# First pair of merge gates interleaved with the sums of blocks, and its block sums moved to GpSimd, in a bidirectional encoder layer on one core

## The chip, the cores and the metric

The kernel runs on one core of a Trainium2 chip. The core has a matrix engine (TensorE: PE, with its weight loads shown apart as PEld), a vector engine (VectorE: DVE), a scalar engine (ScalarE: ACT), a general engine (GpSimd: POOL) and an engine that here issues the DMAs (SyncE: SP). Each of them works through its own list of instructions in order; semaphores hold an instruction back until what it reads is there. SBUF is the on-chip memory that all engines use, PSUM the banks into which the matmuls accumulate. The metric is the device time of one execution in microseconds; the time of a kernel is the median of its runs. The profile is of one execution that the hardware profiler took.

## What is computed

One layer of an encoder with two parallel token mixers, a merge by gates and a SwiGLU block, 1024 tokens (and 16 learned ones in front) of 1024 values, all in float32:

```
h = rmsnorm(h_res, norm1_w[l])
proj = h @ w_in[l]
(q, k, v, z, b_raw, a_raw, sc_b, sc_c, sc_x, gate_a, gate_b) = jnp.split(proj, SPLIT_POINTS, axis=-1)
o_dn = gated_deltanet_bidir(q, k, v, z, b_raw, a_raw, dn_conv_w[l], A_log[l], dt_bias[l], dn_norm_w[l])
y_a = o_dn @ w_branch_dn[l]
y_b = (sc_b * depthwise_conv_centred(sc_c * sc_x, sc_conv_w[l])) @ w_branch_sc[l]
merged = jax.nn.sigmoid(gate_a) * y_a + jax.nn.sigmoid(gate_b) * y_b
h_res = h_res + merged @ w_out[l]
```

The change lies where the columns `z` (the last three of its eight units of 128 columns) and `gate_a`, `gate_b` (the last five of eight units) of `h @ w_in` are computed.

## The kernel before

**Arithmetic.** Every float32 matrix is held as two parts, `hi` and `lo`, and a product takes three matmuls: hi·hi, hi·lo, lo·hi. `split` (L100) makes the parts of a weight: ACT casts the raw tile to `hi` (L101), DVE subtracts to get `lo` (L102). `dense` (L129 to L136) is the plain product of one unit of weights with 512 tokens: 8 blocks of 128 rows, three matmuls each, 24 in all, into one PSUM bank.

**Stages.** The heads of the DeltaNet run first, then the part of the change, then the merge, the output projection and the SwiGLU block. The part of the change starts with three `z` units: `z_rows(h)` (L1496) makes a left and a right half of 512 tokens; for each, 24 matmuls, a tanh on ACT (L1502) and a `scalar_tensor_tensor` on DVE (L1504) that reads the bank and leaves the result in the tile `s`. They are called z0, z1 and z2 here.

Then come the gates, in pairs: pair n takes unit j = 3 + n of `gate_a` and of `gate_b`, for n = 0 to 4. A pair is done as a 2×2 block product with seven block products in place of eight (the scheme of Strassen in Winograd's form). Each block product (`product`, L1434) is 12 matmuls of 128×512. The stationary side is made from weights: the blocks A11, A12 (from the first unit) and A22 (from the second) as they are, and the block sums S1 to S4. The moving side is made from the tokens: B11, B21, B22 as they are, and the sums T1 to T4. Products that are added go into the same bank one after another (`add_to`), and between them ACT copies the bank (L1543 is the copy behind A12·B21 and S2·T2 of a pair, into a tile of four, `s4`).

- `moving_sums` (L1442) makes T1 to T4 from the token tiles `hTh` and `al`. T1 and T2 are formed in the two halves of the tile `mA`, T3 and a helper `d_` in the tile `b3`. DVE does the additions (L1409) and subtractions (L179), ACT the casts to `hi` (L1457), DVE the subtractions to `lo` (L179 too). T4 is formed over T1 once T2 and T3 are done, and its parts are put into `b3`.
- `sums` (L1414) makes S1 to S4 of a pair in place, in the raw weight tiles `rg` and `ru`: one addition (L1416) and three subtractions (L179) of 128×512 on DVE. `stationary2` (L1421) splits them into `mB` (even pairs) or `mA` (odd pairs). A11, A12 are split into `wh`, `wl`, A22 into `w2` (even) or `u_hl` (odd).
- `pair` (L1534) runs the seven products of a pair. For all but the last pair the order is A11·B11, A12·B21, S2·T2, S1·T1, S3·T3, S4·B22, A22·T4.

**Banks.** PSUM has three groups: two banks `pm` (`psm`), three `pe` (`psd`), three `pd` (`pss`). `psany` goes round all of them, `psz` round `pm` and `pe` only. A pair takes one `pd` bank, and two banks of `psz`.

**Order.** From the first `z` unit to the end of pair 0 the program is under a manual schedule for DVE, PE and ACT (`border0`, L1493 to L1617): these three do their work in the order in which it is written, whatever waits. That order is the run of `next(...)` calls at the end of the listing. After it, and for SP and POOL throughout, a scheduler sets the order.

Of the kernel before, what the change touches and what calls it, by code (L numbers as in the profile page):

```python
# [11 lines left out]
AF = mybir.ActivationFunctionType  # L12
# [6 lines left out]
KT = 8  # L19
# [29 lines left out]
def encoder_layer(ctx: ExitStack, tc: tile.TileContext, x, meta, norm1_w, w_in, w_ba,  # L49
# [128 lines left out]
    def sub(out, a, b):  # L178
        nc.vector.tensor_tensor(out=out, in0=a, in1=b, op=ALU.subtract)  # L179
# [856 lines left out]
    with tc.tile_pool(name="st", bufs=1) as st:  # L1036
# [374 lines left out]
    s_hl, u_hl = [None, None], [None, None]  # L1411
    mov = {}

    def sums(rg, ru, s2, s4_, s3, s1):  # L1414
        g0, g1, u0, u1 = rg[:, 0:4], rg[:, 4:8], ru[:, 0:4], ru[:, 4:8]
        nc.vector.tensor_tensor(out=s1, in0=u0, in1=u1, op=ALU.add)  # L1416
        sub(s3, g0, u0)
        sub(s2, s1, g0)
        sub(s4_, g1, s2)

    def stationary2(j, ru, sa, sb, A_):  # L1421

# [19 lines left out]
    def moving_sums():  # L1442

        c = [slice(C0 + META + 512 * i, C0 + META + 512 * i + 512) for i in range(2)]
        f = lambda m: m.bitcast(F32)
        h0, h1 = ([f(hx[0][:, 4 * i:4 * i + 4, cc]) for cc in c] for i in range(2))
        l0, l1, l2 = ([f(t[:, :, cc]) for cc in c] for t in low_tiles)
        for i in range(2):
            for j in range(2):
                mov[f"B{i + 1}{j + 1}"] = hx[0][:, 4 * i:4 * i + 4, c[j]], [hx[1][4 * i + k][:, c[j]] for k in range(4)]  # L1450
        for i, n in enumerate(("T1", "T2", "T3")):
            t = big(f"b{i}", [P, 2, 4, 512])
            mov[n] = t[:, 0], t[:, 1]
# [3 lines left out]
        high = lambda n, t: nc.scalar.copy(mov[n][0], t)  # L1457
# [12 lines left out]
        low_part("T2", t2)  # L1470
        yield
        sub(t3, h1[1], h0[1])
        sub(d_[:, a], l1[1], l0[1][:, a])
        sub(d_[:, b], l2[1], l0[1][:, b])
        add(t3, t3, d_)
        high("T3", t3)
        yield
        sub(t1, h1[0], t2)
        low_part("T3", t3)
        yield  # L1480
        t = big("b3", [P, 2, 4, 512])
# [14 lines left out]
    def z_rows(h):  # L1496

        sz = s4(SEQ)
        for sl in (left, right):
            po = psany()  # L1500
            dense(po, z_units[h - ZH], hx, C0 + META + sl.start, 512)
            nc.scalar.activation(sz[:, sl], po, AF.Tanh, scale=0.5)  # L1502
            yield
            nc.vector.scalar_tensor_tensor(out=sz[:, sl], in0=sz[:, sl], scalar=1.0, in1=po, op0=ALU.add, op1=ALU.mult)  # L1504
        nc.sync.dma_start(z_d[h], sz)
        yield
# [3 lines left out]
    def pair_weights(n, j):  # L1510

        s_hl[n % 2] = big(("mB", "mA")[n % 2], [P, 2, 2, KT, P])
        if n == 0:
            u = big("w2", [P, 2, 4, P])
            u_hl[0] = u[:, 0], u[:, 1]
        elif n == 1:
            u_hl[1] = [tp.tile([P, 4, P], F32R, tag="t2", name=uid("u_hl"), bufs=2) for _ in range(2)]
        gh, gl = wtiles([P, KT, P])
        rg, ru = (rawtile([P, KT, P]) for _ in range(2))
        nc.sync.dma_start(rg, w_in[unit(OGA + j * P)])  # L1520
        nc.sync.dma_start(ru, w_in[unit(OGB + j * P)])
# [5 lines left out]
        def second():  # L1527
            split(*u_hl[n % 2], ru[:, 4:8])
# [3 lines left out]
        return A_, first, second  # L1532

    def pair(n, j, A_, first, second):  # L1534

        last = j == KT - 1
        o1, o2 = s4(), s4()
        bank = pss()
        if not last:
            if n:  # L1540
                first()
            product(bank, A_["A11"], "B11")
            nc.scalar.copy(o1[:, left], bank)  # L1543
            po = psz()
            product(po, A_["A12"], "B21")
            add(o1[:, left], po, o1[:, left])
            half_turn(o1[:, left])
# [4 lines left out]
        bank2 = psz()
        if not last:
            product(bank, A_["S2"], "T2", True)
            nc.scalar.copy(o1[:, right], bank)
            product(bank2, A_["S1"], "T1")
            nc.scalar.copy(o2[:, right], bank2)
            product(bank, A_["S3"], "T3", True)
            add(o2[:, right], bank, o2[:, right])
            half_turn(o2[:, right])  # L1560
            product(bank2, A_["S4"], "B22", True)
            add(o1[:, right], bank2, o1[:, right])
            half_turn(o1[:, right])
            product(bank, A_["A22"], "T4", True)
            nc.scalar.activation(o2[:, left], bank, AF.Tanh, scale=0.5)
        else:
# [421 lines left out]
```

## Time and profile before

| | us |
|---|---|
| median of three runs | 2007.1 |
| the three runs | 2004.61, 2007.71, 2007.1 |
| the profiled execution, its own time | 2003.46 |
| its span (first to last instruction) | 2001.7 |
| PE busy in the span | 1974.2 |
| DVE busy | 1398.8 |
| ACT busy | 837.2 |
| POOL busy | 108.0 |

The span is what the profile covers; the time of an execution has 1.76 us more, which lie outside it. "Busy" is the time in which an engine had at least one instruction running. A timeline row has the start, the duration, the engine, the line, the operation with the tiles it writes and reads, and in brackets the idle time ahead of it with the instruction that ended it. A row of windows has the length of the window, then busy time and instruction count of PE, PEld, DVE, ACT and POOL, the granted clock of TensorE (1.00 is full), the share of the DMA engines and GB/s.

### The profile page before, as it was taken

How to read it: one execution, taken by the hardware profiler on the slowest of the kernel's cores; microseconds unless marked ns; L12 is line 12 of the kernel's file. 1: busy time of each engine (PE TensorE's matmuls, PEld its weight loads, DVE VectorE, ACT ScalarE, POOL GpSimd, SP SyncE). 2: the span in 40 equal slices, each digit the busy share in tenths (PEclk: the TensorE clock that was granted, in tenths of full speed). 3: DMA queues.
4: the chain of work that ended last, by engine and by line, in shares of the span. 5: the costliest groups of instructions: out<-in, count | busy, mean ns of one | idle time of the engine just before them, and what ended most of it. 6: DMA issues, size and time to landing. Idle time of an engine off the chain costs nothing.

```text
span 2001.7 us, 31862 instructions
## 1 busy us (share of the span) xinstructions
PE 1974.2 (99%) x11999; PEld 1720.7 (86%) x11999; DVE 1398.8 (70%) x3020; ACT 837.2 (42%) x1964; POOL 108.0 (5%) x407
## 2 busy tenths in 40 slices
PE   9999999999999999999899999999999999999998
PEld 8999999999999999888688888887888888888887
DVE  6888688888888888844945544469866666656575
ACT  6472354636464646343344221224323333334344
POOL 2011101010101010100000000000000000000000
PEclk9999999999999999999999999999999999999999
DMA  3122221212222212222236743123666345477654
GB/s 133 65 90 74 59 86 59 75 59 75 59 75 59 86 59 65 75 85 91 94 112 239 248 151 112 63 85 107 240 231 216 140 150 188 157 276 244 193 170 172
DMA packets 124689, 251.00 MB, mean 125 GB/s; under 512 B 44981, under 2 KB 46438, under 8 KB 122103
## 3 DMA queue, kind: packets, MB, share of 16 engines
q1 hardware_dynamic: 123959, 247.92, 37.2%
q8 instruction: 94, 1.54, 0.3%
q10 hardware_dynamic: 576, 1.05, 0.1%
q14 instruction: 60, 0.49, 0.1%
HBM read 180.67 MB, written 68.25 MB: 124 GB/s over the span
## 4 chain that ended last, share of the span: by engine, by line
PE 47%; DVE 3%; ACT 1%; issue 1%; DMA 1%; SPq 0%; DVEq 0%; ACTq 0%
PE pd L1440 13%; PE pe L1440 6%; PE pm L1440 4%; PE pe L1894 1%; PE pe L1895 1%; PE pe L1896 1%; PE pd L1894 1%; PE pd L1895 1%; PE pd L1896 1%; PE pd L135 1%; PE pd L134 1%; PE pe L135 1%; PE pe L134 1%; PE pd L136 1%; PE pe L136 1%; PE pm L1895 1%
## 5 line engine op out<-in xcount | busy, mean ns | idle before, releaser
L341 PE MATMUL pm<-hTh,wh 128*128 128x320 f32 (+4 forms) x1264 | 434.2, 349 | 0.4 <-ACT hTh L1103 0.2
L341 PE MATMUL pm<-al,wh 128*128 128x320 f32 (+4 forms) x1264 | 433.6, 348 | 0.0
L341 PE MATMUL pm<-hTh,wl 128*128 128x320 f32 (+4 forms) x1264 | 431.7, 347 | 0.0
L341 PEld LDWEIGHTS pm<-hTh,wh 128*128 128x128 f32 x1264 | 236.7, 188 | 12.6 <-issue 1.3
L341 PEld LDWEIGHTS pm<-hTh,wl 128*128 128x128 f32 x1264 | 237.0, 188 | 10.9 <-issue 0.4
L341 PEld LDWEIGHTS pm<-al,wh 128*128 128x128 f32 x1264 | 236.9, 188 | 10.3
L102 DVE TENSOR_TENSOR al<-raw,ring_h 128x1024 fp32r<-128x1024 f32 x73 | 88.6, 1223 | 64.8 <-ACT ring_h L101 64.4
L101 ACT CAST ring_h<-raw 128x1024 fp32r<-128x1024 f32 x73 | 76.8, 1053 | 107.1 <-PE pe L1896 35.5
L363 DVE SCALAR_TENSOR_TENSOR kq<-ra,wc,kq 128x520 f32<-128x520 f32 x128 | 96.6, 755 | 4.9 <-ACT kq L393 4.0
L990 DVE TENSOR_TENSOR wl<-raw,wh 128x512 fp32r<-128x512 f32 x114 | 77.4, 689 | 31.1 <-ACT wh L993 30.6
L889 ACT ACTIVATE w<-pd,small 128x128 f32<-128x128 f32 x128 | 39.8, 363 | 125.0 <-PE pd L882 124.3
L101 ACT CAST wh<-raw 128x1024 fp32r<-128x1024 f32 x48 | 50.4, 1050 | 77.7 <-PE pd L135 18.7
L500 DVE TENSOR_TENSOR fP<-fP,tm 128x135 f32<-128x135 f32 (+23 forms) x248 | 71.7, 289 | 5.1
L496 DVE TENSOR_TENSOR tm<-fP,fN 128x135 f32<-128x135 f32 (+23 forms) x248 | 71.5, 288 | 4.4
L993 ACT CAST wh<-raw 128x512 fp32r<-128x512 f32 x114 | 67.4, 621 | 3.7 <-issue 3.6
L102 DVE TENSOR_TENSOR wl<-raw,wh 128x1024 fp32r<-128x1024 f32 x48 | 58.5, 1220 | 13.6 <-ACT wh L101 13.4
L1409 DVE TENSOR_TENSOR b<-pd,b 128x512 f32<-128x512 f32 x22 | 15.2, 690 | 66.2 <-PE pd L1440 66.2
L1831 ACT ACTIVATE b<-b 128x512 f32<-128x512 f32 x22 | 13.9, 632 | 113.3 <-DVE b L1409 113.3
L1440 PE MATMUL pd<-b_hl,wh 128*128 128x512 f32 x176 | 54.4, 390 | 0.0
L856 ACT ACTIVATE jk<-NP 128x128 f32<-128x128 f32 x64 | 19.9, 311 | 78.8 <-DVE NP L852 77.7
L1440 PE MATMUL pd<-b,mB 128*128 128x512 f32 x204 | 50.7, 398 | 1.1 <-ACT s L1543 1.1
L876 DVE SCALAR_TENSOR_TENSOR r<-pd,negEG,vS 128x128 f32<-128x128 f32 x120 | 36.7, 345 | 20.9 <-PE pd L866 20.5
(590 smaller groups left out, 4724.6 us busy)
## 6 DMA issues: line engine op xcount, KB each, us to landing
raw<-in_w_in_dram SPq DMA_DIRECT2D x72, 512.0 KB
raw<-in_w_gate_up_dram SPq DMA_DIRECT2D x44, 512.0 KB
sums<-in_w_down_dram SPq DMA_DIRECT2D x22, 512.0 KB
t_d<-sums SPq DMA_DIRECT2D x11, 1024.0 KB
raw<-s_d SPq DMA_DIRECT2D x44, 256.0 KB
raw<-t_d SPq DMA_DIRECT2D x44, 256.0 KB
act_d<-b SPq DMA_DIRECT2D x43, 256.0 KB
raw<-act_d SPq DMA_DIRECT2D x33, 256.0 KB
```

The source lines that it names most:

```text
L101: nc.scalar.copy(hi, src)
L102: nc.vector.tensor_tensor(out=lo, in0=src, in1=hi.bitcast(F32), op=ALU.subtract)
L134: mm(po[:m, :n], wh[:, k, :m], xhk[:, t0:t0 + n], start=(k == 0), stop=False)
L135: mm(po[:m, :n], wh[:, k, :m], xlk[:, t0:t0 + n], start=False, stop=False)
L341: mm(po[:, :n], ww[:, k], f(k)[:, t0:t0 + n], start=i == 0, stop=i == 3 * KT - 1)
L363: nc.vector.scalar_tensor_tensor(out=acc, in0=raw[:, h0 + t:h0 + t + hn], scalar=wc[:, t, col:col + 1], in1=acc, op0=ALU.mult, op1=ALU.add)
L496: nc.vector.tensor_tensor(out=tv, in0=fP[:, 0:r, j:j + 1].broadcast_to([P, r, n]), in1=fN[:, j:j + 1, j + 1:32].broadcast_to([P, r, n]), o ...
L500: nc.vector.tensor_tensor(out=fP[:, 0:r, j + 1:32], in0=fP[:, 0:r, j + 1:32], in1=tv, op=ALU.subtract)
L990: nc.vector.tensor_tensor(out=u[1][1][:, k], in0=u[2][:, k], in1=u[1][0][:, k].bitcast(F32), op=ALU.subtract)
L993: nc.scalar.copy(u[1][0][:, k], u[2][:, k])
L1440: mm(po, x[:, k], y, start=k + i == 0 and not add_to, stop=k == 3 and i == 2, skip_group_check=add_to)
L1895: mm(bank[t], h_[:, c], l_[:, hi], start=False, stop=False)
```

## The change

The diff has four parts.

- **GpSimd.** `sums` takes an engine, and its four operations go to GpSimd for pairs 0 and 1, to DVE for the others. Two of the operations of `moving_sums` (the subtractions of 128×1024 that make `d_` for T3) go to GpSimd as well and are written further ahead, right behind T1's addition.
- **z banks.** `z_rows` takes its banks by `psz` in place of `psany`, so never a `pd` bank.
- **Order within a pair.** S4·B22 comes ahead of S3·T3 in all pairs but the last. The block sums of the weights (`block_sums`) are apart from the split that follows (`second`).
- **Order between the parts.** `pair` becomes a generator that is advanced step by step. A11·B11 and A12·B21 of pair 0, with their copies, stand ahead of T3's parts; S2·T2 to S3·T3 of pair 0 are taken in turn with the parts of T4; the A11 and A12 products of pair 1 come ahead of pair 0's A22·T4; and the manual schedule reaches into pair 1.

The number of products, matmuls, splits and sums is the same.

```
-    def sums(rg, ru, s2, s4_, s3, s1):
+    def sums(rg, ru, s2, s4_, s3, s1, engine=nc.vector):
...
-        nc.vector.tensor_tensor(out=s1, in0=u0, in1=u1, op=ALU.add)
-        sub(s3, g0, u0)
-        sub(s2, s1, g0)
-        sub(s4_, g1, s2)
+        tt = engine.tensor_tensor
+        tt(out=s1, in0=u0, in1=u1, op=ALU.add)
+        tt(out=s3, in0=g0, in1=u0, op=ALU.subtract)
+        tt(out=s2, in0=s1, in1=g0, op=ALU.subtract)
+        tt(out=s4_, in0=g1, in1=s2, op=ALU.subtract)
...
         add(t1, t1, d_)
+        for p_, l_ in ((a, l1), (b, l2)):
+            nc.gpsimd.tensor_tensor(out=d_[:, p_], in0=l_[1], in1=l0[1][:, p_], op=ALU.subtract)
         high("T1", t1)
...
         sub(t3, h1[1], h0[1])
-        sub(d_[:, a], l1[1], l0[1][:, a])
-        sub(d_[:, b], l2[1], l0[1][:, b])
         add(t3, t3, d_)
...
-            po = psany()
+            po = psz()
             dense(po, z_units[h - ZH], hx, C0 + META + sl.start, 512)
...
+        def block_sums():
             split(*u_hl[n % 2], ru[:, 4:8])
             A_["A22"] = u_hl[n % 2]
-            sums(rg, ru, rg[:, 0:4], rg[:, 4:8], ru[:, 0:4], ru[:, 4:8])
-            stationary2(n, ru, rg, ru, A_)
+            sums(rg, ru, rg[:, 0:4], rg[:, 4:8], ru[:, 0:4], ru[:, 4:8], nc.gpsimd if n < 2 else nc.vector)
...
+        else:
+            if n > 1:
+                first()
+                block_sums()
+            product(bank, A_["A11"], "B11")
+            nc.scalar.copy(o1[:, left], bank)
+            po = psz()
+            product(po, A_["A12"], "B21")
+            add(o1[:, left], po, o1[:, left])
+            half_turn(o1[:, left])
+            yield
+            if n:
+                second()
+            bank2 = psz()
+            product(bank, A_["S2"], "T2", True)
+            nc.scalar.copy(o1[:, right], bank)
+            product(bank2, A_["S1"], "T1")
+            nc.scalar.copy(o2[:, right], bank2)
+            yield
+            product(bank2, A_["S4"], "B22", True)
+            add(o1[:, right], bank2, o1[:, right])
+            half_turn(o1[:, right])
+            product(bank, A_["S3"], "T3", True)
+            add(o2[:, right], bank, o2[:, right])
+            half_turn(o2[:, right])
+            yield
+            product(bank, A_["A22"], "T4", True)
+            nc.scalar.activation(o2[:, left], bank, AF.Tanh, scale=0.5)
...
-    pair0 = pair_weights(0, GH)
+    weights0 = pair_weights(0, GH)
     next(z1)
-    pair0[1]()
+    weights0[1]()
+    weights0[2]()
     next(z1)
-    pair0[2]()
+    weights0[3]()
     next(z2)
     next(sums_of_blocks)
     next(z2)
-    next(sums_of_blocks)
-    next(sums_of_blocks)
+    pair0 = pair(0, GH, *weights0)
+    weights1 = pair_weights(1, GH + 1)
+    next(pair0)
     next(z2)
     next(sums_of_blocks)
-    for n, j in enumerate(range(GH, KT)):
-        o1 = pair(n, j, *(pair_weights(n, j) if n else pair0))
-        if n == 0:
-            border0.close()
+    weights1[1]()
+    weights1[2]()
+    next(pair0)
+    next(sums_of_blocks)
+    next(pair0)
+    pair1 = pair(1, GH + 1, *weights1)
+    next(pair1)
+    next(sums_of_blocks)
+    next(pair0)
+    next(pair1)
+    border0.close()
+    for _ in pair1:
+        pass
```

On DVE, before, from the low part of A22 of pair 0 (`w2`) on: between it and the first operation of T3 (the row that writes `b3` from `hTh` alone) stand the four block sums of pair 0 (tiles `raw_2094` and `raw_2095`), the first sums of pair 1 (`raw_2111`, `raw_2112`) with its A22 (`u_hl`), and the low parts of pair 0's S blocks (`mB`).

```order
L102 TENSOR_TENSOR w2_2091_12318<-raw_2095_12322,w2_2091_12318 128x512
L102 TENSOR_TENSOR u_hl_2108_12538<-raw_2112_12542,u_hl_2107_12537 128x512
L1416 TENSOR_TENSOR raw_2095_12322<-raw_2095_12322 128x512
L1416 TENSOR_TENSOR raw_2112_12542<-raw_2112_12542 128x512
L179 TENSOR_TENSOR raw_2095_12322<-raw_2094_12321,raw_2095_12322 128x512
L179 TENSOR_TENSOR raw_2112_12542<-raw_2111_12541,raw_2112_12542 128x512
L179 TENSOR_TENSOR raw_2094_12321<-raw_2095_12322,raw_2094_12321 128x512
L179 TENSOR_TENSOR raw_2094_12321<-raw_2094_12321 128x512
L102 TENSOR_TENSOR mB_2090_12317<-raw_2094_12321,mB_2090_12317 128x1024
L102 TENSOR_TENSOR mB_2090_12317<-raw_2095_12322,mB_2090_12317 128x1024
L179 TENSOR_TENSOR b3_2083_12244<-hTh_127 128x2048
L179 TENSOR_TENSOR b3_2083_12244<-al_2_125,al_1_124 128x1024
```

On DVE, with the change, from the same row on:

```order
L102 TENSOR_TENSOR w2_2091_12320<-raw_2095_12324,w2_2091_12320 128x512
L1505 SCALAR_TENSOR_TENSOR s4_2088_12292<-s4_2088_12292,pe_2096_12328 128x512
L102 TENSOR_TENSOR mB_2090_12319<-raw_2094_12323,mB_2090_12319 128x1024
L102 TENSOR_TENSOR mB_2090_12319<-raw_2095_12324,mB_2090_12319 128x1024
L179 TENSOR_TENSOR b3_2083_12244<-hTh_127 128x2048
L1409 TENSOR_TENSOR b3_2083_12244<-b3_2083_12244 128x2048
L1505 SCALAR_TENSOR_TENSOR s4_2097_12368<-s4_2097_12368,pm_2098_12369 128x512
L1409 TENSOR_TENSOR s4_2107_12434<-pm_2110_12450,s4_2107_12434 128x512
L1505 SCALAR_TENSOR_TENSOR s4_2097_12368<-s4_2097_12368,pe_2099_12399 128x512
L179 TENSOR_TENSOR mA_2082_12243<-hTh_127,mA_2082_12243 128x2048
L179 TENSOR_TENSOR b2_2081_12242<-b3_2083_12244,b2_2081_12242 128x2048
```

No block sum is left there, and pair 1's are gone from this place; the low parts of `mB` follow the split of `w2` with one z operation between. T3 has lost its two subtractions, the sum of pair 0's A11 and A12 products (into `s4_2107`) stands between the two halves of z2, and T4's first subtraction (into `mA`) ahead of T3's low part (into `b2`).

On POOL, which had nothing in this part before, the last instructions of its work are now the two subtractions for T3 and then the block sums of pair 0 and of pair 1:

```order
L1464 TENSOR_TENSOR b3_2083_12244<-al_2_125,al_1_124 128x1024
L1464 TENSOR_TENSOR b3_2083_12244<-al_3_126,al_1_124 128x1024
L1417 TENSOR_TENSOR raw_2095_12324<-raw_2095_12324 128x512
L1418 TENSOR_TENSOR raw_2095_12324<-raw_2094_12323,raw_2095_12324 128x512
L1419 TENSOR_TENSOR raw_2094_12323<-raw_2095_12324,raw_2094_12323 128x512
L1420 TENSOR_TENSOR raw_2094_12323<-raw_2094_12323 128x512
L1417 TENSOR_TENSOR raw_2106_12431<-raw_2106_12431 128x512
L1418 TENSOR_TENSOR raw_2106_12431<-raw_2105_12430,raw_2106_12431 128x512
L1419 TENSOR_TENSOR raw_2105_12430<-raw_2106_12431,raw_2105_12430 128x512
L1420 TENSOR_TENSOR raw_2105_12430<-raw_2105_12430 128x512
```

Each reads two tiles in SBUF; the first sum waits for the splits of pair 0's raw tiles, and the low parts of `mB` on DVE wait, by way of ACT's casts, for the last of the four.

On ACT, before, from the tanh of z2's left half to the first copy of pair 0 (`b2` is T3, `b3` T4, `wh_2109` and `wh_2119` are the first parts of pairs 1 and 2):

```order
L1502 ACTIVATE s4_2097_12366<-pd_2098_12367 128x512
L101 CAST wh_2109_12539<-raw_2111_12541 128x1024
L101 CAST wh_2119_12659<-raw_2121_12661 128x1024
L1457 CAST b2_2081_12242<-b3_2083_12244 128x2048
L1502 ACTIVATE s4_2097_12366<-pd_2099_12399 128x512
L1457 CAST b3_2100_12427<-mA_2082_12243 128x2048
L1543 COPY s4_2101_12434<-pd_2103_12436 128x512
```

and with the change, from the casts of pair 0's S blocks on:

```order
L101 CAST mB_2090_12319<-raw_2094_12323 128x1024
L101 CAST mB_2090_12319<-raw_2095_12324 128x1024
L1503 ACTIVATE s4_2097_12368<-pm_2098_12369 128x512
L1458 CAST b2_2081_12242<-b3_2083_12244 128x2048
L1503 ACTIVATE s4_2097_12368<-pe_2099_12399 128x512
L1572 COPY s4_2107_12434<-pd_2109_12436 128x512
```

The copy of pair 0 (L1543 before, L1572 now) stands ahead of T4's cast, and no cast of a later pair's weights stands ahead of T3's.

More of the change, by code (lines that the diff above doesn't have):

```diff
@@ L1527, in second, with pair @@
         def second():
+            stationary2(n, ru, rg, ru, A_)
+        def block_sums():
             split(*u_hl[n % 2], ru[:, 4:8])
             A_["A22"] = u_hl[n % 2]
-            sums(rg, ru, rg[:, 0:4], rg[:, 4:8], ru[:, 0:4], ru[:, 4:8])
-            stationary2(n, ru, rg, ru, A_)
-        return A_, first, second
-    def pair(n, j, A_, first, second):
+            sums(rg, ru, rg[:, 0:4], rg[:, 4:8], ru[:, 0:4], ru[:, 4:8], nc.gpsimd if n < 2 else nc.vector)
+        return A_, first, block_sums, second
+    def pair(n, j, A_, first, block_sums, second):
         last = j == KT - 1
-        o1, o2 = s4(), s4()
+        o1, o2 = outs[n] = s4(), s4()
         bank = pss()
[L1539 to L1547, printed above, removed]
         if last:
             first()
-        if n:
+            block_sums()
             second()
[L1552 to L1566, printed above, removed]
+            bank2 = psz()
             product(bank, A_["S2"], "T2")
@@ L1586, in pair @@
             half_turn(o1[:, right])
+        else:
+            if n > 1:
+                first()
+                block_sums()
+            product(bank, A_["A11"], "B11")
[7 more added lines that the diff above has]
+                second()
+            bank2 = psz()
+            product(bank, A_["S2"], "T2", True)
[12 more added lines that the diff above has]
+            nc.scalar.activation(o2[:, left], bank, AF.Tanh, scale=0.5)
         nc.sync.dma_start(ta_d[j], o1)
         nc.sync.dma_start(tb_d[j], o2)
-        return o1
+        yield
+    outs = {}
     sums_of_blocks = moving_sums()
@@ L1609, in encoder_layer @@
     next(z2)
-    next(sums_of_blocks)
-    next(sums_of_blocks)
+    pair0 = pair(0, GH, *weights0)
+    weights1 = pair_weights(1, GH + 1)
+    next(pair0)
     next(z2)
     next(sums_of_blocks)
-    for n, j in enumerate(range(GH, KT)):
-        o1 = pair(n, j, *(pair_weights(n, j) if n else pair0))
-        if n == 0:
-            border0.close()
+    weights1[1]()
[11 more added lines that the diff above has]
+        pass
+    for n, j in enumerate(range(GH + 2, KT), 2):
+        for _ in pair(n, j, *pair_weights(n, j)):
+            pass
+    o1 = outs[KT - 1 - GH][0]
     warm2 = keep.tile([P, 1], F32, name="warm2")
```

## The prediction

> **What bounds the kernel now.** I read the page's list of busy times first, then the windows around the changed part, then the timelines of PE, DVE and ACT there.
>
> ```profile
> PE 1974.2 (99%) x11999; PEld 1720.7 (86%) x11999; DVE 1398.8 (70%) x3020; ACT 837.2 (42%) x1964; POOL 108.0 (5%) x407
> ```
>
> PE sets the end. A change that keeps the matmuls can only gain where PE stands or runs slowly.
>
> ```profile
> 945.96:1010.06 64.10, 54.52 (x219) 43.13 (x218) 52.87 (x44) 23.88 (x27) 0.00 (x0) 0.92 0.28 93
> 1010.06:1091.00 80.94, 80.94 (x357) 66.66 (x356) 40.77 (x49) 36.64 (x51) 0.00 (x0) 1.00 0.46 164
> 980.00:1000.00 20.00, 11.57 (x39) 8.32 (x37) 19.53 (x15) 8.26 (x9) 0.00 (x0) 0.83 0.20 66
> 989.80:996.50 6.70, 5.12 (x12) 3.80 (x12) 6.70 (x5) 2.40 (x2) 0.00 (x0) 0.50 0.00 0
> 1000.00:1003.40 3.40, 2.96 (x7) 2.39 (x8) 3.40 (x4) 1.30 (x2) 0.00 (x0) 0.52 0.19 75
> ```
>
> From the first z matmul to pair 0's S4·B22 PE is busy 54.52 of 64.10 us; behind that it is full. Between 980 and 1000 DVE is busy 19.53 of 20: DVE is the bound there. Two stretches of some 3.4 and 6.7 us have half the clock.
>
> ```profile
> 945.96 0.39 PE L134 MATMUL pm<-hTh,wh 128*128 128x512 f32 x1
> 951.40 0.39 PE L134 MATMUL pe<-hTh,wh 128*128 128x512 f32 x1
> 968.07 0.50 PE L134 MATMUL pd<-hTh,wh 128*128 128x512 f32 x1 [0.19 <-ACT wh L101]
> 969.33 0.51 PE L136 MATMUL pd<-hTh,wl 128*128 128x512 f32 x1 [0.53 <-DVE wl L102]
> 979.90 0.39 PE L1440 MATMUL pd<-hTh,wh 128*128 128x512 f32 x1
> 991.38 0.77 PE L1440 MATMUL pd<-hTh,wh 128*128 128x512 f32 x1 [5.88 <-DVE s L1504]
> 998.56 0.50 PE L1440 MATMUL pd<-hTh,wh 128*128 128x512 f32 x1 [1.85 <-DVE s L1504]
> 1000.43 4.33 PE L1440 MATMUL pd<-b,mB 128*128 128x512 f32 x12 [1.14 <-ACT s L1543]
> 1010.06 0.39 PE L1440 MATMUL pe<-hTh,mB 128*128 128x512 f32 x1
> ```
>
> A half of z is 24 matmuls in 951.40 − 945.96 = 5.44 us, so 0.227 us each. The 218 matmuls (count of weight loads) are worth 49.4 us; they take 64.1. **At stake are 14.7 us**, 0.7% of the time: waits 0.19 + 0.53 + 5.88 + 1.85 + 1.14 = 9.6; half clock 5.12 − 12·0.227 = 2.4 and 2.96 − 7·0.227 = 1.4; the last 1.3 is start-up behind the waits, which I count into them below. 5.88 and 1.85 are `pd` banks that z2 holds until DVE comes to L1504.
>
> **The change part by part.** The z banks leave `pd`, so those two waits go, and PE has other work while DVE makes T3. Nothing runs less: ten operations leave DVE for POOL, and POOL's cost is not free for DVE:
>
> ```profile
> L1118 POOL TENSOR_TENSOR wl<-raw,wh x4: 1274/1287/1720, 15.6 to 25.0; 128x512 fp32r<-128x512 f32 x4
> L587 POOL TENSOR_TENSOR Nm<-Nm,Dm x8: 212/548/707, 103.7 to 767.7; 16x16 f32<-16x16 f32 x8
> 23.33 2.98 POOL L1118 TENSOR_TENSOR wl<-raw,wh 128x512 fp32r<-128x512 f32 x2 [5.19 <-ACT wh L1117]
> 20.28 0.22 DVE L167 SCALAR_TENSOR_TENSOR ss<-ss 128x1 f32<-128x1 f32 x1
> 22.62 1.29 DVE L1089 SCALAR_TENSOR_TENSOR xr<-xr,ss,w1row 128x1024 f32<-128x1024 f32 x1
> 24.07 0.99 DVE L167 SCALAR_TENSOR_TENSOR ss<-ss 128x1 f32<-128x1 f32 x1
> 25.10 1.22 DVE L168 SCALAR_TENSOR_TENSOR ss<-ss 128x1 f32<-128x1 f32 x1
> ```
>
> A 128×512 subtraction on POOL takes 1.27 us. For 128×1024 the slope between L587's shortest (16 wide, 0.21) and L1118's gives 0.21 + 1008·(1.27 − 0.21)/496 = 2.37; twice 1.27 is the upper end. In the group the longest took 1.72: it started while DVE's L1089, which reads two SBUF tiles, was running, and ended 1.14 us behind that. In turn DVE's one-column L167, 0.22 when alone, took 0.99 and ended at 25.06, where POOL's first operation ended; L168 took 1.22 to 26.32, where POOL's second ended (23.33 + 2.98 = 26.31). So an operation of POOL and one of DVE with both inputs in SBUF shut each other out, and they took turns. Most of DVE's work here has both inputs in SBUF.
>
> By the Trainium skill, GPSIMD Engine Reference, 3.1 Elementwise, a GpSimd addition 2048 wide takes 4497 ns; an estimate from that is 2.25 us at 1024, and the next sum would be 0.25 less by it. The 1.27 us row is of this chip and I keep the slope.
>
> ```profile
> 957.63 2.29 DVE L1409 TENSOR_TENSOR mA<-mA,b 128x2048 f32<-128x2048 f32 x1
> 959.96 2.29 DVE L179 TENSOR_TENSOR mA<-hTh,mA 128x2048 f32<-128x2048 f32 x1
> 962.28 2.36 DVE L1409 TENSOR_TENSOR mA<-mA,al 128x1024 f32<-128x1024 f32 x2
> 964.68 1.92 ACT L1457 CAST b<-mA 128x2048 fp32r<-128x2048 f32 x1 [2.81 <-DVE mA L1409]
> 966.98 1.04 ACT L101 CAST wh<-raw 128x1024 fp32r<-128x1024 f32 x1
> ```
>
> *(a) T3's subtractions on POOL.* They may start when T1's addition ends (959.92). DVE's next, T2's subtraction, is at the lock first (to 962.25). Then by turns: POOL to 964.6, DVE's addition to 965.8, POOL to 968.2, DVE's second to 969.4. T2 is thus ready at 969.4, not 964.64: 4.75 late. On ACT behind T2's cast stands the cast of z2's weights, which ends at 968.02 now; it moves by the same to 972.7. z1 runs out at 967.9, so PE stands 4.9 us, then 0.6 for the low part as today (0.53). It is over 3.4 us, and 5.88 us was followed by half a clock: another 1.4 (as in the 3.4 us stretch). **Loss 6.9**; z2 ends at 985.5 in place of 979.9. If POOL came last instead, (a) would be the 0.7 of today; if both came ahead of T2, the same 6.9.
>
> ```profile
> 974.33 0.69 DVE L102 TENSOR_TENSOR w<-raw,w 128x512 fp32r<-128x512 f32 x1
> 975.53 1.29 DVE L1416 TENSOR_TENSOR raw<-raw 128x512 f32<-128x512 f32 x2
> 976.74 1.89 DVE L179 TENSOR_TENSOR raw<-raw,raw 128x512 f32<-128x512 f32 x3
> 978.66 0.69 DVE L179 TENSOR_TENSOR raw<-raw 128x512 f32<-128x512 f32 x1
> 979.38 2.00 ACT L101 CAST mB<-raw 128x1024 fp32r<-128x1024 f32 x2 [5.66 <-DVE raw L179]
> 980.47 2.36 DVE L102 TENSOR_TENSOR mB<-raw,mB 128x1024 fp32r<-128x1024 f32 x2 [1.11 <-ACT mB L101]
> 982.74 2.29 DVE L179 TENSOR_TENSOR b<-hTh 128x2048 f32<-128x2048 f32 x1
> 988.35 2.29 DVE L1409 TENSOR_TENSOR b<-b 128x2048 f32<-128x2048 f32 x1
> 990.55 0.68 DVE L1504 SCALAR_TENSOR_TENSOR s<-s,pd 128x512 f32<-128x512 f32 x1
> 990.67 1.90 ACT L1457 CAST b<-b 128x2048 fp32r<-128x2048 f32 x1 [4.09 <-DVE b L1409]
> 999.81 0.58 ACT L1543 COPY s<-pd 128x512 f32<-128x512 f32 x1
> ```
>
> *(b) Pair 0's sums on POOL.* DVE ends `w2`'s low part at 975.0 now. In the changed order the 4.75 stand ahead of it, and less z work: I get 979.0. POOL's four sums, each on the one before, take 4·1.27 and small gaps, 5.3: to 984.3. DVE has nothing else: the low parts of `mB` stand at the head of its list and wait for ACT's first cast (half of 2.00), so DVE idles from 979.6 to 985.5. That gives up what the move saves (four of 0.65, and pair 1's share that is put off). Then 2.3 (`mB`) and T3's two operations, 2.2 + 2.3, to 992.3. ACT: T3's cast 1.9, z2's tanh 0.5, pair 0's copy 0.58 (it stands behind the cast): 995.3. S2·T2 adds into the bank that this copy reads. PE, from 985.5 on A11·B11 and A12·B21 (24·0.227 = 5.4), is done at 991.0. **Loss 4.3**, against 5.88 + 1.85 + 1.14 before. Whether the clock falls is open, 0 or 1.4; I take half, 0.7.
>
> By the Trainium skill, TensorE: Matmul & The Clock Gate, Part 1, the clock halves after an idle window of about 3.4 us whose start is free-running; a 4.3 us wait may hold a whole window or not. That gives the same two ends; no run here shows the phase.
>
> *(c) Behind it.* S4·B22 now follows S1·T1 in the same bank, with ACT's copy (0.58) between and no product as cover: 0.8. Pair 1's S2·T2 meets the casts of its `mA` late, 1.0, and its S4·B22 0.7. T4 is hidden: its first matmul needs only `hi`, and pair 2's A11 covers the rest. Pairs 2 and 3 have products between. **Loss 2.5**; below nothing it cannot be, since PE stands nowhere there now, and without ACT's delays it is 0.
>
> *Free.* Pair 1's four sums on POOL lie in DVE's T4 stretch and push T4 by some 2.4, under the products of pair 0 and 1 (without them, 2.4 more). The DMA order hardly moves, and the loads are far ahead.
>
> Sum: 6.9 + 4.3 + 0.7 + 2.5 + 0.3 (start-ups) = **14.7 lost, against 14.7 before**. Bounds: POOL's price 1.13 to 1.5 times moves it by −1 to +5.5; (a) without turns −6.2; the clock −0.7 to +0.7. The span stays 2001.7 and the profiled time 2003.5. This execution lies 3.6 below the median of the runs shown, so on the median I say 2007.1.
>
> **The rivals.** *A: DVE and POOL pass each other.* POOL waits while DVE's list is full, or the lock does not hold for these tiles. For: the small POOL operations elsewhere wait little; against: L167 and L168 above. (a) falls to 0.7, T3 is earlier, but (b) grows, since its sums still take 5.3: loss 10.4, time 2007.1 − 4.3 = **2002.8**. The Trainium skill, Perfetto Trace Analysis, Optimizing Scalar/DVE Operations, says that moves between these two might not help as they share a port: it speaks against A, as do the rows.
>
> *B, slower: POOL's operations are dear.* L1118's rows are of whole tiles; the new ones read column slices of wide tiles and write in place. At 1.5 times the price (a) grows by 2·1.2 and (b) by 4·0.64 through T3, S2·T2 and, at 6.9 us of standing, the second half clock: +2.4 +2.5 +0.7: **2012.7**. It decides from about 1.3 times on. For it: the group's longest, 1.72. Against: that row is a wait.
>
> *C: more is gained.* If DVE's spare time also lets T3 come before pair 0's A12 ends, PE stands only at the start of z2: 14.7 − 6.9 = 7.8 less: **1999.3**. Against: POOL's sums alone outlast the cover.
>
> *Nothing moves* is excluded: the order rows show it.
>
> **How the numbers follow.** Forecast 0.48, A 0.20, B 0.22, C 0.10. Within 0.2%, 4 us, about what can be told from no change, lies the forecast alone; faster is A and C, 0.30; slower B, 0.22. The range runs from below A's to B's price, 2001.5 to 2012.7, leaving out C and B's upper part. The forecast's own range is 2003.2 to 2011.
>
> **What would show it.** (a): a wait of 4 to 5.5 us at z2's first matmul on ACT's `wh`, T2's additions on DVE each with POOL's subtraction ahead. (b): 4 to 5 us at pair 0's S2·T2 on ACT's copy, DVE idle 5 to 6 us ahead of `mB`, POOL at 1.27 us each. (c): three waits of under 1 us. Wrong: z2 starting at 968, POOL beyond 1.6 us, or PE full from 945 to 1030.

## The result, and the profile after

| | median us | runs | ratio to before, 95% interval |
|---|---|---|---|
| before | 2006.69 | 20 | |
| changed | 2008.48 | 20 | 1.0007 (1.0001 to 1.0013) |

The change makes the kernel 1.8 us slower. That is less than the 0.2% within which the prediction looked for it, but its interval leaves no change out. The profiled execution took 2010.23 us with a span of 2008.5; it lies 1.75 above the median, where the one of before lay 3.2 below its own, so the two spans differ by more than the medians.

In the page's list of busy times of the changed kernel DVE has lost only 2.4 us, though ten operations left it, and POOL has gained 19.9:

```profile
PE 1978.9 (99%) x11999; PEld 1722.9 (86%) x11999; DVE 1396.4 (70%) x3010; ACT 837.2 (42%) x1964; POOL 127.9 (6%) x417
```

As a yardstick that other parts of the program do not touch, I take "the part": from the first z matmul to the A11·B11 of the last pair, which is the fifth of that pair's products. These are the same 528 matmuls in both kernels: 144 of z, 84 in each of the pairs 0 to 3, and 48 of the last pair. (Where an expectation says "pair 4's first product", this point is meant.) The end of it in the timeline of PE, before (its start, 945.96, is shown in the prediction):

```profile
1080.44 0.39 PE L1440 MATMUL pe<-hTh,wh 128*128 128x512 f32 x1
```

and in the changed kernel its start, the waits in it and its end:

```profile
947.08 0.39 PE L134 MATMUL pe<-hTh,wh 128*128 128x512 f32 x1
973.58 0.79 PE L134 MATMUL pm<-hTh,wh 128*128 128x512 f32 x1 [4.58 <-ACT wh L101]
996.34 5.49 PE L1441 MATMUL pd<-b,mB 128*128 128x512 f32 x12 [3.58 <-ACT s L1572]
1005.65 0.50 PE L1441 MATMUL pe<-hTh,mB 128*128 128x512 f32 x1 [0.68 <-ACT s L1584]
1026.46 2.58 PE L1441 MATMUL pd<-b,mA 128*128 128x512 f32 x10 [0.69 <-DVE mA L102]
1084.89 0.39 PE L1441 MATMUL pe<-hTh,wh 128*128 128x512 f32 x1
```

The part took 1080.44 − 945.96 = 134.5 us before and 1084.89 − 947.08 = 137.8 in this execution; 528·5.44/24 = 119.7 of it is work, so the loss went from 14.8 to 18.1. Outside the part the two executions differ by another 3.5 us (2001.7 − 134.5 and 2008.5 − 137.8); the profiles of all experiments, with and without the change, lie between these two values, so that difference is not put down to the change. The waits on z2's `pd` banks are gone. In their place stand the wait of z2's first matmul for its weights and the wait of pair 0's S2·T2 for ACT's copy. The same kernel's timelines of POOL, DVE and ACT show what is behind them:

```profile
961.39 7.69 POOL L1464 TENSOR_TENSOR b<-al,al 128x1024 f32<-128x1024 f32 x2 [133.79 <-DVE mA L1409]
980.00 1.29 POOL L1417 TENSOR_TENSOR raw<-raw 128x512 f32<-128x512 f32 x1 [10.91 <-DVE w L102]
984.10 1.28 POOL L1420 TENSOR_TENSOR raw<-raw 128x512 f32<-128x512 f32 x1
1003.82 2.18 POOL L1417 TENSOR_TENSOR raw<-raw 128x512 f32<-128x512 f32 x1 [18.44 <-DVE u_hl L102]
```

```profile
963.53 6.64 DVE L1409 TENSOR_TENSOR mA<-mA,al 128x1024 f32<-128x1024 f32 x2
986.50 2.36 DVE L102 TENSOR_TENSOR mB<-raw,mB 128x1024 fp32r<-128x1024 f32 x2 [5.98 <-ACT mB L101]
```

```profile
985.42 2.00 ACT L101 CAST mB<-raw 128x1024 fp32r<-128x1024 f32 x2 [9.45 <-POOL raw L1420]
995.71 0.58 ACT L1572 COPY s<-pd 128x512 f32<-128x512 f32 x1
```

T2's two additions on DVE took 6.64 us (2.36 before): each had one of POOL's subtractions ahead of it. POOL's sums took 1.29 us each while DVE had nothing to do, up to 2.18 where DVE was at work, and DVE stood 5.98 us ahead of `mB`, behind the four of them. The last thing to read is the clock, in windows of 3.41 us that are laid so that it changes at their edges:

```profile
968.52:971.93 3.41, 0.48 (x3) 0.06 (x1) 3.41 (x2) 1.73 (x1) 0.57 (x1) 0.99 0.00 0
971.93:975.34 3.41, 1.72 (x3) 1.00 (x4) 2.82 (x4) 3.41 (x7) 0.00 (x0) 0.50 0.00 0
975.34:978.75 3.41, 3.41 (x9) 2.62 (x8) 3.41 (x4) 0.63 (x2) 0.00 (x0) 0.51 0.59 192
992.33:995.74 3.41, 0.43 (x2) 0.01 (x1) 1.65 (x2) 2.32 (x3) 0.00 (x0) 1.00 0.04 16
995.74:999.15 3.41, 2.81 (x7) 2.23 (x8) 2.83 (x3) 2.65 (x6) 0.00 (x0) 0.50 0.21 85
999.15:1002.56 3.41, 3.41 (x10) 2.64 (x9) 3.41 (x3) 1.51 (x2) 0.00 (x0) 0.50 0.18 71
```

Behind each wait the clock was halved for two such windows, 6.8 us, not one.

### The profile page after: what moved, and what is told of

Its sections match the earlier page's. It is cut to its first block, busy times and chain, and to the rows that moved or that the text cites. A ratio compares the mean times of both kernels' runs of the same rounds, so it can differ in the third digit from the quotient of the medians.

```text
span 2008.5 us, 31868 instructions
## 1 busy us (share of the span) xinstructions
PE 1978.9 (99%) x11999; PEld 1722.9 (86%) x11999; DVE 1396.4 (70%) x3010; ACT 837.2 (42%) x1964; POOL 127.9 (6%) x417
## 4 chain that ended last, share of the span: by engine, by line
PE 45%; DVE 3%; DMA 1%; issue 1%; ACT 1%; POOL 0%; SPq 0%; DVEq 0%; POOLq 0%; ACTq 0%
PE pd L1441 13%; PE pe L1441 6%; PE pm L1441 4%; PE pe L1919 1%; PE pe L1918 1%; PE pe L1920 1%; PE pd L1919 1%; PE pd L1918 1%; PE pd L1920 1%; PE pd L134 1%; PE pe L134 1%; PE pd L136 1%; PE pe L135 1%; PE pe L136 1%; PE pd L135 1%
## 5 line engine op out<-in xcount | busy, mean ns | idle before, releaser
L102 DVE TENSOR_TENSOR al<-raw,ring_h 128x1024 fp32r<-128x1024 f32 x73 | 88.5, 1221 | 64.9 <-ACT ring_h L101 64.5
L102 DVE TENSOR_TENSOR wl<-raw,wh 128x1024 fp32r<-128x1024 f32 x48 | 58.6, 1221 | 15.9 <-ACT wh L101 15.6
L856 ACT ACTIVATE jk<-NP 128x128 f32<-128x128 f32 x64 | 19.9, 311 | 78.7 <-DVE NP L852 77.7
```

The lines of the kernel that those rows point to most:

```text
L102: nc.vector.tensor_tensor(out=lo, in0=src, in1=hi.bitcast(F32), op=ALU.subtract)
```

## The experiments

Theory S, as it stood from the prediction on: GpSimd and DVE take turns, S2·T2 stands at the end of DVE's list, and the new order gains what the work on GpSimd gives back. (The letters of theories and rivals in the expectations are their own, and not the A, B, C of the prediction.) All times are compared with runs of before on the same chip; "the part" is that of the run's own profile.

| run | median us | before us | ratio, interval | part us |
|---|---|---|---|---|
| T3 on DVE | 2005.93 | 2006.16 | 0.9998 (0.9989 to 1.0007) | 134.8 |
| sums on DVE | 2003.54 | 2006.16 | 0.9983 (0.9974 to 0.9992) | 132.5 |
| nothing on GpSimd | 2003.17 | 2006.16 | 0.9983 (0.9975 to 0.9992) | 131.7 |
| PE kept busy | 2006.56 | 2006.16 | 1.0000 (0.9991 to 1.0010) | 136.4 |
| z banks alone | 2007.33 | 2006.18 | 1.0004 (0.9995 to 1.0013) | 136.3 |
| T3 behind T2 | 2006.33 | 2006.18 | 1.0000 (0.9991 to 1.0009) | 135.3 |
| S3 first, one execution | 2005.43 | 2006.18 | | 134.2 |
| S3 first, timed | 2007.11 | 2006.85 | 0.9999 (0.9990 to 1.0007) | 134.8 |
| copy ahead | 1999.31 | 2006.18 | 0.9965 (0.9953 to 0.9977) | 127.7 |
| copy ahead, S3 first | 1997.51 | 2006.85 | 0.9956 (0.9942 to 0.9969) | 128.1 |

**T3's subtractions back on DVE**

```
-        for p_, l_ in ((a, l1), (b, l2)):
-            nc.gpsimd.tensor_tensor(out=d_[:, p_], in0=l_[1], in1=l0[1][:, p_], op=ALU.subtract)
...
+        sub(d_[:, a], l1[1], l0[1][:, a])
+        sub(d_[:, b], l2[1], l0[1][:, b])
         add(t3, t3, d_)
```

> The changed kernel with T3's two 128x1024 subtractions back on DVE, in their old place (1.22 us each); pair 0's and pair 1's block sums stay on GpSimd. Theory S (GpSimd and DVE take turns, so the work put on GpSimd gives back what the new order gains): T2's additions take 2.4 us again in place of 6.6, z2 starts within 0.5 us of z1's end (4.6 us wait gone); the wait moves to pair 0's S2*T2 and grows from 3.6 to about 7, since T3 is only some 2.3 us earlier (4.75 less on DVE ahead of T2, 2.3 more in T3). One stretch of half clock in place of two. Net about 2 to 5 us less than the changed kernel: 2003 to 2006. Rival R (the new order is what costs, GpSimd is free): as the changed kernel, 2008 to 2009.

The timeline of its PE:

```profile
968.46 0.50 PE L134 MATMUL pm<-hTh,wh 128*128 128x512 f32 x1 [0.62 <-ACT wh L101]
993.55 4.69 PE L1441 MATMUL pd<-b,mB 128*128 128x512 f32 x12 [7.67 <-ACT s L1572]
```

z2's wait is 0.62 in place of 4.58, and S2·T2's has grown from 3.58 to 7.67. Of the 4 us taken from one wait most came back in the next: counted from the first z matmul S2·T2 started 1.6 us earlier (993.55 − 945.92 = 47.63, against 49.26). The part is 3.0 us shorter; most of the other 1.4 is the clock, since S2·T2's twelve matmuls took 4.69 us here and 5.49 in the changed kernel, although the wait ahead of them was longer.

**The block sums back on DVE**

```
-            sums(rg, ru, rg[:, 0:4], rg[:, 4:8], ru[:, 0:4], ru[:, 4:8], nc.gpsimd if n < 2 else nc.vector)
+            sums(rg, ru, rg[:, 0:4], rg[:, 4:8], ru[:, 0:4], ru[:, 4:8], nc.vector)
```

> The changed kernel with the block sums of pairs 0 and 1 back on DVE (four of 0.65 us each); T3's subtractions stay on GpSimd. Theory S: the 4.6 us wait at z2 and its half clock stay; DVE's idle time ahead of mB falls from 6.0 to about 3, S2*T2 of pair 0 starts 2.9 us earlier, its wait falls to under 1 us, too short for the clock to fall, so 3 us of slow matmuls go as well. About 5 us less than the changed kernel: 2003 to 2004. Rival R: as the changed kernel, 2008 to 2009, or slower as DVE has 5.2 us more to do.

```profile
972.65 0.80 PE L134 MATMUL pm<-hTh,wh 128*128 128x512 f32 x1 [4.85 <-ACT wh L101]
992.93 3.04 PE L1441 MATMUL pd<-b,mB 128*128 128x512 f32 x12 [0.82 <-ACT s L1572]
```

In its timeline of PE z2 still waits 4.85, with a slow clock behind it, and yet S2·T2 waits only 0.82 and runs its twelve matmuls in 3.04 us, at the full clock. The 5 us that were expected came: this is the dearer half of the move to GpSimd. Of the 5.3 us in the part, 2.2 are S2·T2's earlier start (992.93 − 945.88 = 47.05, against 49.26), and nearly all the rest is the slow clock that did not come. Taking turns is not what costs at this place: in the changed kernel POOL ran pair 0's four sums at 1.29 us each while DVE stood idle behind them.

**Nothing on GpSimd** (both edits together)

> The changed kernel with nothing moved to GpSimd: T3's subtractions and all block sums on DVE, so only the banks of z and the order of the work are changed. Theory S: z2 without its wait, pair 0's S2*T2 about 5 us earlier than in the changed kernel, with one wait of 4 to 5 us and one stretch of half clock. 5 us less than the changed kernel and 3 to 5 less than before: 2002 to 2004. Rival R (the new order gains nothing): 2007 to 2009.

```profile
968.42 0.50 PE L134 MATMUL pm<-hTh,wh 128*128 128x512 f32 x1 [0.40 <-ACT wh L101]
990.89 4.34 PE L1441 MATMUL pd<-b,mB 128*128 128x512 f32 x12 [5.04 <-ACT s L1572]
```

With banks and order alone the kernel is 3.0 us faster than before. The ratio goes from 1.0007 to 0.9983, so the move to GpSimd costs about 0.0024·2006 = 4.8 us, more than the rest of the change gains. The rival, that the new order gains nothing, falls. The two halves do not add up (by the ratios 1.8 and 4.8 us, against 4.8 for both), since a wait that goes at z2 is found again at S2·T2.

**PE kept busy.** 32 matmuls that nobody reads stand in the two waits.

```
+    def busy(n):
+        if "bank" not in fill:
+            fill["bank"] = pss()
+        w_ = mov["T1"][0]
+        for i in range(n):
+            mm(fill["bank"], w_[:, i % 4, :P], w_[:, i % 4], start=True, stop=True)
...
+            if h == H - 1 and sl is left:
+                busy(18)
             dense(po, z_units[h - ZH], hx, C0 + META + sl.start, 512)
...
+            if n == 0:
+                busy(14)
             product(bank, A_["S2"], "T2", True)
```

> The changed kernel with matmuls added whose result nobody reads: 18 ahead of z2's first matmul and 14 ahead of pair 0's S2*T2, into a bank of their own and from tiles that are long ready (18 and 14 times 0.227 = 4.1 and 3.2 us, inside the waits of 4.6 and 3.6 us). They move nothing but keep PE at work. Theory C (the part of the loss that was mis-sized is the clock: 6.7 us at half clock behind each of the two waits, 2.5 and 3.1 us): the granted clock stays at 1.00 from 960 to 1010, z2's and S2*T2's matmuls start every 0.227 us, the part from z to pair 4 is 5.5 us shorter; 2003 to 2006. Rival (the slow matmuls come from something else than the wait ahead, or the added ones delay): clock at 0.5 behind the waits as before, 2008 to 2010.

Windows of this run:

```profile
968.50:972.00 3.50, 2.95 (x14) 2.10 (x12) 2.89 (x4) 3.38 (x4) 0.00 (x0) 1.00 0.00 0
972.00:977.00 5.00, 4.46 (x18) 3.39 (x19) 5.00 (x5) 2.40 (x4) 0.00 (x0) 1.00 0.37 120
991.90:995.40 3.50, 1.36 (x7) 0.76 (x6) 1.16 (x3) 2.82 (x3) 0.00 (x0) 0.98 0.00 0
995.40:998.80 3.40, 3.40 (x10) 2.68 (x9) 3.40 (x4) 3.03 (x4) 0.00 (x0) 0.52 0.39 157
```

and its S2·T2:

```profile
994.77 4.61 PE L1441 MATMUL pd<-b,mB 128*128 128x512 f32 x12 [2.14 <-ACT s L1583]
```

At z2 the clock stayed at 1.00, so its fall there was the wait's doing. At S2·T2 it still fell: z2 ended sooner, the wait grew past the 14 matmuls, and PE was busy 1.36 of 3.5 us ahead of it. Half the theory is shown, and the gain was 1.5 us of the part, not 5.5; the time of 2006.56 us lies above the 2003 to 2006 that were expected. The reason is worth more than the gain: S2·T2 started 49.3 us behind the first z matmul (994.77 − 945.45), as in the changed kernel. The slow clock at z2 cost nothing; it only shortened the next wait.

**The z banks alone,** on the kernel before:

```
-            po = psany()
+            po = psz()
             dense(po, z_units[h - ZH], hx, C0 + META + sl.start, 512)
```

> The kernel before with one line changed: the z rows take their banks from pm and pe, never a pd bank. Theory S (S2*T2 of pair 0 is held by the copy that stands behind T3's and T4's casts on ACT, and those by DVE; the banks only decide where PE waits): the waits of 5.9 and 1.9 us on z2's pd banks go, pair 1's A11 starts at once and then waits some 2.5 us for its low part, but S2*T2 still starts within 0.5 us of 54.5 us behind the first z matmul; the wait there grows from 1.1 to about 6. Time within 1.5 us of before. Rival B (the banks are what the new order gains by): the 7.7 us of waits are gained, 1999 to 2001.

PE, then ACT:

```profile
988.67 0.50 PE L1440 MATMUL pd<-hTh,wl 128*128 128x512 f32 x1 [1.29 <-DVE wl L102]
1000.61 5.49 PE L1440 MATMUL pd<-b,mB 128*128 128x512 f32 x12 [8.07 <-ACT s L1543]
```

```profile
998.17 1.90 ACT L1457 CAST b<-mA 128x2048 fp32r<-128x2048 f32 x1 [4.93 <-DVE mA L1409]
999.98 0.58 ACT L1543 COPY s<-pd 128x512 f32<-128x512 f32 x1
```

The bank waits of 7.7 us are gone and nothing is gained: S2·T2 starts where it did (1000.61 − 945.81 = 54.8; 54.5 before), behind a copy that stands behind T4's cast. The banks decided where PE waits, not how long.

**T3 behind T2.** GpSimd's subtractions are held back by a one-column operation that reads T2.

```
+        for p_, l_ in ((a, l1), (b, l2)):
+            e_ = t2[:, 1 if p_ is a else 3, 0:1]
+            nc.gpsimd.tensor_tensor(out=d_[:, p_.start, 0:1], in0=e_, in1=e_, op=ALU.subtract)
+            nc.gpsimd.tensor_tensor(out=d_[:, p_], in0=l_[1], in1=l0[1][:, p_], op=ALU.subtract)
```

> The changed kernel with GpSimd's two subtractions for T3 held back until T2 is made: a one-column GpSimd operation that reads T2 stands ahead of each, in the column that is then overwritten. Theory S (the turns with GpSimd are paid on DVE wherever they fall, and S2*T2 is at the end of DVE's list): z2 starts without its 4.6 us wait, T2's additions take 2.4 us; the turns fall on the low parts of T1 and T2 and z2's weights instead, S2*T2 is only 1 us earlier and its wait grows to 7 or 8 us. One stretch of half clock less work is lost at z2: 1 to 3 us less than the changed kernel, 2005 to 2007. Rival (the place of the subtractions was the mistake, z2's wait is what costs): 5 to 7 us less than the changed kernel, 2001 to 2003.

DVE, POOL and PE:

```profile
963.47 2.36 DVE L1409 TENSOR_TENSOR mA<-mA,al 128x1024 f32<-128x1024 f32 x2
```

```profile
965.96 4.32 POOL L1471 TENSOR_TENSOR b<-al,al 128x1024 f32<-128x1024 f32 x1
971.49 4.32 POOL L1471 TENSOR_TENSOR b<-al,al 128x1024 f32<-128x1024 f32 x1
```

```profile
993.92 5.44 PE L1441 MATMUL pd<-b,mB 128*128 128x512 f32 x12 [4.71 <-ACT s L1574]
```

T2's additions are back at 2.36, z2 has no wait of 4 us, and S2·T2 still starts at 47.2 (993.92 − 946.76), 2.1 us earlier than in the changed kernel where 1 was expected. The turns have moved, with POOL's subtraction now waiting behind a DVE operation of 2.28 us. That the place of the subtractions was the mistake is not what the time shows: some 2 us by the medians, 1.4 by the ratios, not 5 to 7.

**S3 ahead of S4** in the changed kernel, in one execution and then in eleven:

```
+            product(bank, A_["S3"], "T3", True)
+            add(o2[:, right], bank, o2[:, right])
+            half_turn(o2[:, right])
             product(bank2, A_["S4"], "B22", True)
...
-            product(bank, A_["S3"], "T3", True)
```

> The changed kernel with S3*T3 ahead of S4*B22 again. Theory S: the wait of 0.7 us at S4*B22 of pair 0 on ACT's copy of the same bank goes, at S3*T3 there is at most 0.3 for T3's low part; 0.5 to 0.8 us less in the part, nothing that the time shows. Rival: S4 ahead covers T3's late parts, so S3*T3 waits over 1 us here.

> The changed kernel with S3*T3 ahead of S4*B22, once more, now timed: if the order of the two costs what its one look suggests, some 2 us in all (0.7 in pair 0, the rest in pairs 1 to 3) less than the changed kernel: 2005.5 to 2007. If the look's 3.65 us were all the clock's phase: 2008 to 2009.

PE in the single execution, then in the profiled one of the eleven:

```profile
995.11 4.61 PE L1441 MATMUL pd<-b,mB 128*128 128x512 f32 x12 [3.22 <-ACT s L1572]
1022.97 2.58 PE L1441 MATMUL pd<-b,mA 128*128 128x512 f32 x10 [0.69 <-DVE mA L102]
1079.90 0.39 PE L1441 MATMUL pe<-hTh,wh 128*128 128x512 f32 x1
```

```profile
995.60 5.14 PE L1441 MATMUL pd<-b,mB 128*128 128x512 f32 x12 [4.33 <-ACT s L1572]
1023.99 2.58 PE L1441 MATMUL pd<-b,mA 128*128 128x512 f32 x10 [0.68 <-DVE mA L102]
1080.93 0.39 PE L1441 MATMUL pe<-hTh,wh 128*128 128x512 f32 x1
```

The wait of 0.68 at S4·B22 is gone and S3·T3 shows none. The part was 3.65 and 3.1 us shorter than in the changed kernel's profile, more than that wait. Some of it is the clock: S2·T2's twelve matmuls took 4.61 and 5.14 us, 5.49 in the changed kernel. The two executions are of one kernel, so what the clock costs there differs from one execution to the next. In the single one it was halved behind S2·T2's wait for one window, not two:

```profile
995.40:998.80 3.40, 3.40 (x9) 2.63 (x9) 3.40 (x4) 2.99 (x4) 0.00 (x0) 0.53 0.39 157
```

The rest is mostly in pairs 1 to 3: from the end of pair 1's wait (L102 `mA`) to the end of the part it is 56.9 us in both (1079.90 − 1022.97, 1080.93 − 1023.99), 58.4 in the changed kernel (1084.89 − 1026.46). Five other runs with S4 first, those that show the same row, have 58.2 to 58.4 there. So S4 first costs 1.2 to 1.5 us in pairs 1 to 3 of these profiles; why was not examined. In the time itself the two kernels are not told apart (0.9999 with its interval against 1.0007 with its own; 2005.5 to 2007 was expected, 2007.11 measured).

**The copy ahead.** Nothing on GpSimd, and T3's cast on ACT written behind pair 0's first copy.

```
         add(t3, t3, d_)
+        yield
         high("T3", t3)
...
             nc.scalar.copy(o1[:, left], bank)
+            if n == 0:
+                yield
             po = psz()
...
     next(pair0)
+    next(sums_of_blocks)
+    next(pair0)
     next(z2)
```

> Everything on DVE as in the run without GpSimd, and pair 0's first copy and the products behind it written ahead of T3's cast on ACT (T3's additions stay where they are on DVE). Theory S (S2*T2 waits for a copy that is ready but stands behind T3's cast): S2*T2 follows A12*B21 with no wait, so 4.5 us and its half clock go; some 2.5 us come back at S4*B22, whose copy is queued behind T3's cast. 3 to 5 us less than without GpSimd (2003.2): 1998 to 2000. Rival (T3 later holds S3*T3, so the wait only moves on): 2002 to 2004.

ACT's copy in the run with nothing on GpSimd, the same copy here, and PE here:

```profile
990.26 0.58 ACT L1572 COPY s<-pd 128x512 f32<-128x512 f32 x1
```

```profile
982.89 0.59 ACT L1573 COPY s<-pd 128x512 f32<-128x512 f32 x1 [2.12 <-PE pd L1441]
```

```profile
985.41 2.88 PE L1441 MATMUL pd<-b,mB 128*128 128x512 f32 x12
992.61 0.50 PE L1441 MATMUL pe<-hTh,mB 128*128 128x512 f32 x1 [1.59 <-ACT s L1587]
```

The copy now waits only for PE, S2·T2 has no wait, and the first one of pair 0 is at S4·B22 (1.59, where some 2.5 were expected). The median is 1999.31 against 2006.18, 0.35% faster than before and 3.9 us below the run without GpSimd, inside what was expected. One of its six executions took 3969.36 us; nothing here explains it, the ratio leaves it out, and without it the median is 1999.27.

**The copy ahead and S3 first in pairs 1 to 3**

```
-            product(bank2, A_["S4"], "B22", True)
...
+            if n == 0:
+                product(bank2, A_["S4"], "B22", True)
...
             product(bank, A_["S3"], "T3", True)
...
+            if n:
+                product(bank2, A_["S4"], "B22", True)
```

> The run with the copy ahead (nothing on GpSimd, pair 0's copy ahead of T3's cast), and in pairs 1 to 3 S3*T3 ahead of S4*B22 again; pair 0 keeps S4 first, since its T3 is late. From the part's length in the run with S3 first (2.3 us less behind pair 0 than the clock explains) I expect 1 to 2 us less than with the copy ahead alone: 1997 to 1999, the part from the first z matmul to pair 4's first product 126 to 127 us (127.7 there). Rival (S4 ahead costs nothing in pairs 1 to 3): 1999 to 2000, 127.7 us.

The median is the lowest of all, 1997.51, but its interval overlaps that of the run before it, and the part was not shorter (128.1). Pair 1's S2·T2 in the run before it, then here, and a window of this run:

```profile
1015.06 2.56 PE L1441 MATMUL pd<-b,mA 128*128 128x512 f32 x10 [1.15 <-DVE mA L102]
```

```profile
1014.94 4.14 PE L1441 MATMUL pd<-b,mA 128*128 128x512 f32 x10 [1.15 <-DVE mA L102]
1015.00:1019.00 4.00, 4.00 (x11) 3.17 (x12) 3.36 (x4) 0.00 (x0) 0.00 (x0) 0.57 0.69 226
```

Eleven matmuls took 4 us behind two waits of 1.2 at pair 1's `mA`: 1.5 us of slow clock that the run before it did not have in the same place behind the same waits. This hides what S3 first gains in the part: from this row to the end of the part it is 58.5 us, and 56.9 without the slow clock (4.14 − 2.56 = 1.6), as in the two runs above. In the time the gain stays open.

## Why the prediction was right or wrong

- **What bounds the part.** Right: S2·T2's start is set by DVE's list, through T3 and the copy behind its cast. The bank waits were only its shape, as the banks alone showed. With the copy ahead S2·T2 waited for neither, so it is the copy's place behind T3's cast, and not T3 itself, that ties it to DVE.
- **Turns between GpSimd and DVE.** Right, and rival A falls: T2's additions took 4.3 us more (6.64 − 2.36), and the prediction had T2 4.75 late. The Trainium skill, SBUF — State Buffer, SBUF: two separate sides, calls it an exclusive lock held for a whole instruction against a DVE operation with two inputs in SBUF; the trace agrees.
- **POOL's price.** Right, and rival B falls: 1.28 to 1.29 us against 1.27 where DVE was idle.
- **(a) and (b).** z2's wait 4.58 (predicted 4.9), DVE idle 5.98 ahead of `mB` (5.9), S2·T2's wait 3.58 (4.3). S2·T2 started 49.26 us behind the first z matmul; the prediction's sum has 995.3 − 945.96 = 49.3. The clock behind z2's wait was under-priced too, two slow windows for a term of 1.4, but that only shortened the next wait: the run that keeps PE busy took the fall away and S2·T2 started at 49.3 all the same.
- **(c).** Waits 0.68 and 0.69 against 0.8 and 1.0. Pair 1's S4·B22 was charged 0.7, and pairs 2 and 3 were called covered; by the profiles S4 ahead of S3 costs 1.2 to 1.5 us in these three pairs. The term was 0.5 to 0.8 too small.
- **The step that failed is the price of the clock at S2·T2**, "0 or 1.4; I take half, 0.7". From S2·T2's start to the end of the part 1084.89 − 996.34 = 88.55 us passed for 360 matmuls, 360·5.44/24 = 81.6 of work: 6.9 lost, where the prediction had 0.7 + 2.5 + 0.3 = 3.5. Of the 3.4 us too much some 2 are the clock: S2·T2's twelve matmuls took 5.49 us, and 3.04 in the run with the sums on DVE, where the clock did not fall; the slow window went on behind them. The rest is what (c) lacked, and small gaps.
- **Why that price was wrong.** Its ends were "no fall" and the 3.40 us row (1.4), while the trace of before had, behind the 5.88 us wait, the 6.70 us row that cost 2.4. No run that waited 2.1 to 8.1 us at S2·T2 went without a fall: the twelve matmuls took 4.34 to 5.49 us, 1.3 to 2.5 more than 3.04. Nor did the price follow the length of the wait, as the rows above show: 4.34 us behind a wait of 5.04 and 4.69 behind 7.67, but 5.44 behind 4.71, and 5.49 behind both 3.58 and 8.07. It goes by where the wait ends within the windows of 3.41 us (last section), and that differs between executions. So the term was a range from 1.3 to 2.5, with no 0 in it.
- **The forecast.** "No change" at 2007.1 is off by the 1.8 us that the medians show. The account above is of one execution, whose part was 3.3 us longer than that of before's. How the 1.8 divide between the clock and (c) is not shown, since the clock's share differs from one execution to the next and the changed kernel has one trace only.
- **C**, that more is gained, fell for this change: T3 did not come before pair 0's A12 was done. The size that it named was reached in another way, with nothing on GpSimd and the copy ahead of T3's cast: 6.9 us.

## What to carry to other kernels

When a list of one engine is the bound, a wait that is removed ahead of its end is paid again at its end: count from the start of the last thing that waits for that list, and let the waits in between fall where they will. Work is not taken off that engine by moving it to a neighbour that needs twice the time, if the two take turns or if the list then stands still behind the moved work; here both happened, and the second was the dearer. Where a copy only stands in a wrong place of a queue, a change of order gains more. Price a stall of the matrix engine with the slow clock that follows it, and as a range: here stalls of 2.1 to 8.1 us were followed by 1.3 to 2.5 us of slow matmuls in the next product, in no order of their length, and two executions of one kernel differed by 0.5.

## What the runs showed of the hardware

- How long the clock stays down: a window of 3.41 us in which PE was busy 0.43 or 0.48 us, and one of 3.50 with 1.36 (in the run that keeps it busy), were followed by half the clock, one busy 2.95 of 3.50 was not. At half the clock, a window with 1.72 or 2.81 us of work was followed by another one at half; a full one was followed by 1.00, and so was the one with 2.96 of 3.40 in the kernel before (1000.00 to 1003.40, in the prediction). So a wait that ends inside a slow window costs the rest of that window, and the next one as well where too little of it is left for work. The slow stretches of the changed kernel start at 971.93 and 995.74, 23.81 us apart, which is seven windows of 3.40, as if the windows ran on whatever PE does. The Trainium skill, TensorE: Matmul & The Clock Gate, Part 1, has the window, free-running, and the return after a busy one; these rows agree.
- GpSimd and DVE took turns, and neither starved the other. In the run with T3 behind T2 a GpSimd subtraction of 128×1024 was recorded at 4.32 us, of which some 2 are its wait for the DVE operation of 2.28 us ahead; in the changed kernel DVE's two additions took 4.3 us more in turn, some 2 each.
